# Two-byte halves of y made at the gating, with GpSimd subtracting and loading the first weights of the last projection

## The chip, the cores and the metric

The kernel runs on one core of a Trainium2 chip. The metric is device time in microseconds, the median of several executions.

## The reference

Two pre-norm residual layers over x (1024 tokens by 1024 features), then a last RMSNorm. Layer 0 is a gated linear recurrence, layer 1 an attention with a forget gate, 16 heads of 64. The change lies in layer 1:

```python
def fox_mixer(h, w_in, b_f, w_out):
    u = h @ w_in                       # q, k, v, gate (1024 each) and f_logit (16)
    cum = jnp.cumsum(jax.nn.log_sigmoid(f_logit), axis=1)
    ...
    logits = einsum(q, k) * scale + (cq - ck)      # causal
    p = jax.nn.softmax(logits, axis=-1)
    o = einsum(p, v)
    y = o * jax.nn.silu(gate)
    return y @ w_out                   # added to x, then rms_norm
```

## The kernel before

One function, `trunk`, writes the whole program; a scheduler with a timeline of its own then settles each engine's order. Features lie along the partitions (128 rows), tokens along the free dimension, in two halves of 512, called c = 0 and 1. Products of nearly four-byte accuracy are made by TensorE from pairs of narrower numbers: each operand is a high part (the number rounded) and a low part (what the rounding lost), and a product is three matmuls, high by high, low by high, high by low. In layer 1 the parts are two-byte (FP16) with scales worked out ahead.

Layer 0 takes the first 470 us or so and isn't touched. Layer 1 goes head by head (`for hd in range(HEADS)`, the loop behind `drain(fill)`); two heads make a pair, since 2 x 64 rows fill the partitions. In a head:

- `maxima(hd, c)` makes the logits `S` for blocks of 128 queries; VectorE adds the mask and takes the extreme (line 1086), ScalarE does the exponential and the high part of the probabilities `pp`, VectorE the low part (1099), and SyncE's queue transposes `pp` to `pT` by DMA (1101).
- `weigh(hd, c)` multiplies `pT` by the values into `O`, and ScalarE and VectorE put the sum into `yo` (1134), four-byte, two buffers by turns.
- `gated(hd, c)`, after the second head of a pair, multiplies `yo` by the gate `sg` on VectorE (1145). For pairs 0 to 5 the product goes to `kept_y`, twelve four-byte tiles under the tag `hl` (16 places); pairs 6 and 7 keep it in `yo`.

Between these, strings such as `"1..1..1..1..0.0"` say at each step whether the next piece is one of the attention (`0`, `1`), of the values (`v`, `w`) or of `fill` (`.`), a stream of large projections: `play(units)` makes units of 24 matmuls for keys, queries and gates. Each unit fills one of the two PSUM banks under the tag `g` (tiles `gps`), which is scaled by VectorE (783) and used: a gate unit by a tanh on ScalarE and a multiply on VectorE (1055, tile `sg`), a key or query unit by a copy and a subtract (909, tile `qkl`). The bank is free again after that.

From head 12 on `fill` holds the last gate units (`last_g`) and then the last projection. `partial(todo)` makes, for each of 8 blocks db of 128 output features and each half c, a unit of 18 matmuls `ops` over pairs 0 to 5; pairs 6 and 7 are added at the end in `turned`. A unit needs:

- the two-byte halves of `y`. `split_loaded` makes them from `kept_y` during the last gate unit and the first units: `split_16`, one scaled cast on ScalarE and one VectorE operation (1175) for each of the twelve tiles, into new places under the tag `hh`, the places of the normed input;
- the block's weights: `split_out(db)` loads them (256 KB and 128 KB) through `load16`, which shares three places `wf` (and SyncE's queue, line 69) with all other weights, and casts them with `cast16` (ScalarE, then VectorE at 738) into `w`;
- the residual block, loaded from DRAM by GpSimd's queue (1236) into the place that `home(c, db)` gives: `xh`, under `hl`, for c = 0; `xp` or `xh` elsewhere for c = 1. VectorE adds the product to it (1239). A copy of one element by GpSimd (1234) holds the next load back until the block before last has been added, and three `xp` blocks are stored again (1241).

`late()` loads and casts the weights of pairs 6 and 7, `turned` transposes the sum, adds the last products and applies the final norm (line 1305, tile `res`).

Of the kernel before, what the change touches and what calls it, by code (L numbers as in the profile page):

```python
# [11 lines left out]
F32 = mybir.dt.float32  # L12
F32R = mybir.dt.float32r
BF16 = mybir.dt.bfloat16
FP16 = mybir.dt.float16
TOP = 32768.0
AF = mybir.ActivationFunctionType
ALU = mybir.AluOpType

P = 128  # L20
SEQ = 1024
HALF = 512
KT = 8
# [20 lines left out]
def trunk(ctx: ExitStack, tc: tile.TileContext, xt, w0, wg, wo0, pc, gn, gf, w1, wv, wf, bf, wo1, out):  # L44
    nc = tc.nc
# [6 lines left out]
    hpool = ctx.enter_context(pool("hT", 16))  # L52
# [155 lines left out]
    with nullcontext(ExitStack()) as l0:  # L208
# [43 lines left out]
        first = ([], [])  # L252
        early = [weights(w0[0], lo_eng=nc.vector), weights(w0[NB], lo_eng=nc.gpsimd)]
        k = 0
# [315 lines left out]
        total_o, unit_o, scale_o, scale_y, inv_o, eps_o, most, gain = (outs[:, i : i + 1] for i in range(8))  # L570
# [100 lines left out]
        for h, cs in enumerate(halves):  # L671
            y = [tuple(z[:, cs] for z in p) for p in ys[-2:]]
# [3 lines left out]
            for d0 in range(0, KT, 4):  # L676
# [6 lines left out]
                for db, o in enumerate(pts, d0):  # L683
                    mm3(o, wl[db][1], y[1], False, True)
                    x = xs[h][db]
# [28 lines left out]
    with ExitStack() as l1:  # L714
# [7 lines left out]
        seen = [None]  # L722

        def load16(src, shape, b):

            wt = loaded(shape)
            for part, sl in src:
                fetch(wt[:, :, sl], part)
            return wt, b

        def cast16(wt, b, scale=None):

            scale = scales[:, b : b + 1] if scale is None else scale
            n = wt.shape[1]
            both = wpool.tile([P, 2, *wt.shape[1:]], FP16, tag=next(slots), name="w16")
            hi, lo = both[:, 0], both[:, 1]
            cast_last[0] = nc.scalar.activation(hi, wt, AF.Copy, scale=scale)
            nc.vector.scalar_tensor_tensor(lo, wt, scale, hi, ALU.mult, ALU.subtract)
            return [(hi[:, k], lo[:, k]) for k in range(n)]
# [144 lines left out]
        sgs = {}  # L884
        yos = {}
        y1 = [{}, {}]
        kept_y = [[hpool.tile([P, HALF], F32, tag="hl", name="y") for pair in range(6)] for c in range(2)]
        wo = {}

        kqw = {}  # L890
# [246 lines left out]
        def gated(hd, c, sub=slice(0, HALF)):  # L1137

            if hd % 2 == 0:
                return  # L1140
            pair = hd // 2
            yo = to = yos[pair, c][:, sub]
            if pair < 6:
                to = kept_y[c][pair][:, sub]
            nc.vector.tensor_tensor(
                to, yo, sgs[pair][:, c * HALF + sub.start : c * HALF + sub.stop], ALU.mult
            )
            if hd == 15:
                split_y(c, pair, yo, sub)

# [17 lines left out]
        def pair_of_y(c, pair):  # L1168
            both = hpool.tile([P, 2, HALF], FP16, tag="hh", name="y16")
            y1[c][pair] = both[:, 0], both[:, 1]  # L1170
            return y1[c][pair]

        def split_16(y, yh, yl):
            to_hi(yh, y, nc.scalar, scale=scale_y)
            nc.vector.scalar_tensor_tensor(yl, y, scale_y, yh, ALU.mult, ALU.subtract)
# [2 lines left out]
            yh, yl = (z[:, sub] for z in (pair_of_y(c, pair) if sub.start == 0 else y1[c][pair]))  # L1178
            split_16(y, yh, yl)

        def high_y(c):
            for pair in range(6):
                pair_of_y(c, pair)
            yield from ()

        def split_loaded(c):
            for pair in range(6):
                y = kept_y[c][pair]
                split_16(y, *y1[c][pair])
                if pair % 2:  # L1190
                    yield

        def beside(steps, first, more):

            for i, _ in enumerate(steps):
                if i >= first:
                    next(more, None)
                yield

        def split_out(db):  # L1200
            if db < KT and db not in wo:
                wo[db] = []
                for k, n in ((0, 4), (4, 2)):
                    wo[db] += cast16(*load16([(wo1[db, :, k : k + n], slice(0, P))], (n, P), None), scale_o)

        def first_out():
            split_out(0)
# [3 lines left out]

        def home(c, db):
            if c == 0:
                x = hpool.tile([P, HALF], F32, tag="hl", name="xh")
            elif db < 3:
                return rpool.tile([P, HALF], F32, tag="R", name="xp")
            elif db < 7:
                x = at.tile([P, HALF], F32, tag="wv", name="xh", bufs=4)
            else:
                x = at.tile([P, HALF], F32, tag="wvf", name="xh", bufs=1)  # L1220
            homes[c, db] = x
            return x
# [153 lines left out]
        for hd in range(HEADS):  # L1376
            pair = hd // 2
            if hd % 2 == 0:
                if hd < 12:
                    fill = play(next(fills))  # L1380
                elif hd == 12:
                    todo = [(db, c) for c in range(2) for db in range(2)]
                    todo += [(db, c) for db in range(2, KT) for c in range(2)]
                    splits = [split_loaded(c) for c in range(2)]
                    fill = chain(
                        play(next(fills)),
                        play(last_g[0]),
                        high_y(0),
                        first_out(),
                        beside(play(last_g[1]), 1, splits[0]),  # L1390
                        high_y(1),
                        beside(partial(todo), 3, splits[1]),
                        last_gains(),
                        turned(0, 0),
                        turned(0, 1),
                    )
            elif pair < 6:
                fill = play(next(fills))
            first, second = LAST if hd > 11 else START if hd == 0 else ORDER
            if hd in (4, 8):  # L1400
                first, second = OPEN
            if hd == HEADS - 1:
                first = "1..1.0.1.0.1..."
            side = chain(pieces(hd + 1, 0, 0), pieces(hd + 1, 0, 1)) if hd else iter(())
            run(first, weigh(hd, 0), maxima(hd, 1), fill=fill, side=side, vals=vals, wvals=wvals)
            drain(side)
            if hd == HEADS - 1:
                break
            if hd == 14:
                with tc.issue_after(seen[0].ins):  # L1410
                    split_y(1, 6, yos[6, 1])
            gated(hd, 0)
            side = chain(pieces(hd + 2, 1, 0), pieces(hd + 2, 1, 1))
            if hd == 14:
                side = chain(side, late())
            if hd % 4 == 3 and hd < 11:
                wvals, second = value_weights(hd // 4 + 2), TURN
            run(second, weigh(hd, 1), maxima(hd + 1, 0), fill=fill, side=side, vals=vals, wvals=wvals)
            if hd % 4 == 3 and hd < 11:
                drain(vals)  # L1420
                vals = values_beside(hd // 4 + 2)
            drain(side)
            gated(hd, 1)
            if hd == 13:
                with tc.issue_after(seen[0].ins):
                    split_y(0, 6, yos[6, 0])
            if hd < 12:
                drain(fill)
# [81 lines left out]
```

## Time and profile before

| | |
|---|---|
| median of 3 runs | 1020.6 us (1019.57 to 1020.7) |
| the profiled execution's own time | 1016.93 us |
| its span, first to last instruction | 1015.2 us |
| mean granted clock of TensorE | 0.999 |
| PE / DVE / ACT / POOL busy | 995.4 / 788.4 / 669.1 / 110.4 us |

PE is TensorE's matmuls, PEld its weight loads, DVE is VectorE, ACT ScalarE, POOL GpSimd, SP SyncE; a q behind the name is that engine's queue. An arrow to the left in a row reads "waits for" where two engines are named, and "made from" where two tiles are. L with a number is a line of the kernel; matmuls, ScalarE's operations and SyncE's loads are issued by helpers and carry the helper's line (72, 60, 69), so they are told apart by their tiles.

### The profile page before, as it was taken

The page shows a single profiled execution, that of the slowest core. Times are in us where ns is not written, and L with a number is a line of the kernel's source. Part 1 is how long each engine was busy: PE and PEld are TensorE (multiplying, and loading weights), DVE is VectorE, ACT ScalarE, POOL GpSimd, SP SyncE. Part 2 cuts the span into 40 slices and gives each one's busy share as a digit, 9 for nine tenths or more (in the row PEclk, how much of TensorE's full clock was granted, in tenths as well). Part 3 has the DMA queues.
Part 4 walks back from the last instruction along what each step waited for, and adds up shares of the span by engine and source line. Part 5 has one row for each costly group of instructions (what it writes and reads, how often), then busy time and mean ns, then how long its engine had stood idle before and what let it go on. Part 6 is the DMA issues. An engine that isn't in the chain of part 4 may idle for free. (4 is left out here: it accounts for less than half of the span.)

```text
span 1015.2 us, 15117 instructions
## 1 busy us (share of the span) xinstructions
PE 995.4 (98%) x5100; PEld 655.3 (65%) x5100; DVE 788.4 (78%) x1500; ACT 669.1 (66%) x1219; POOL 110.4 (11%) x104
## 2 busy tenths in 40 slices
PE   9999999999999999999999999999999999999997
PEld 6787778888888888776545555555555555444454
DVE  7689585586567557898687988988898878995875
ACT  8469855657657567576684667776667666873655
POOL 1310221222122122000200000000010000001200
PEclk9999999999999999999999999999999999999999
DMA  7211443243334333244366687977688677777954
GB/s 256 62 51 48 126 140 97 91 133 103 124 106 131 96 107 113 70 148 137 85 157 124 122 151 147 193 152 150 130 202 136 138 160 150 154 180 185 231 101 167
DMA packets 219629, 135.88 MB, mean 134 GB/s; under 512 B 162080, under 2 KB 186464, under 8 KB 219552
## 3 DMA queue, kind: packets, MB, share of 16 engines
q1 hardware_dynamic: 216912, 126.27, 51.5%
q0 software_dynamic: 2640, 8.65, 3.1%
q8 instruction: 40, 0.66, 0.3%
q14 instruction: 37, 0.30, 0.1%
HBM read 75.16 MB, written 9.37 MB: 83 GB/s over the span
## 5 line engine op out<-in xcount | busy, mean ns | idle before, releaser
L72 PE MATMUL gps<-h,w 128*128 128x512 f16 x1152 | 268.0, 379 | 0.0
L72 PEld LDWEIGHTS <-w 128*128 128x128 f16 x1440 | 139.9, 98 | 156.3 <-issue 6.8
L60 ACT ACTIVATE p<-p,m 128x128 f32<-128x128 f32 (+7 forms) x128 | 98.9, 772 | 84.1 <-DVE m L1086 75.4
L114 POOL TENSOR_TENSOR wl<-wf,wh 128x512 fp32r<-128x512 f32 x46 | 82.0, 1791 | 315.9 <-ACT wh L60 258.5
L1086 DVE CUSTOM_DVE_ANT_0 p<-S,mask,vsq 128x128 f32<-128x128 f32 (+7 forms) x128 | 103.6, 810 | 14.6 <-PE S L72 14.2
L1099 DVE SCALAR_TENSOR_TENSOR pp<-p,sums,pp 128x128 f16<-128x128 f32 (+7 forms) x128 | 103.4, 812 | 12.2 <-ACT pp L60 11.7
L60 ACT ACTIVATE pp<-p,sums 128x128 f16<-128x128 f32 (+7 forms) x128 | 97.9, 768 | 20.1 <-ACT p L60 14.4
L60 ACT ACTIVATE wsf<-wsf 128x512 f32<-128x512 f32 (+1 forms) x81 | 50.5, 625 | 60.5 <-DMA wsf<-in_w 33.0
L72 PEld LDWEIGHTS <-h 128*128 128x128 f16 x768 | 74.8, 98 | 21.0 <-ACT h L60 1.3
L72 PE MATMUL S<-T,U 128*128 128x512 f16 (+4 forms) x384 | 83.4, 327 | 0.1
L72 PE MATMUL ops<-yh,wh 128*128 128x512 f32 x192 | 77.2, 402 | 1.6 <-ACT yh L60 0.9
L72 PE MATMUL ups<-hh,wh 128*128 128x512 f32 x192 | 76.3, 398 | 1.0 <-ACT hh L60 0.8
L72 PE MATMUL ups<-hl,wh 128*128 128x512 f32 x192 | 76.2, 397 | 0.2 <-DVE hl L275 0.2
L72 PE MATMUL ops<-yh,wl 128*128 128x512 f32 x192 | 75.7, 394 | 0.8 <-DVE wl L114 0.8
L72 PE MATMUL ups<-hh,wl 128*128 128x512 f32 x192 | 75.6, 394 | 0.8 <-POOL wl L114 0.8
L72 PE MATMUL gps<-hh,wh 128*128 128x512 f32 x192 | 75.8, 395 | 0.0
L72 PE MATMUL gps<-hh,wl 128*128 128x512 f32 x192 | 75.5, 393 | 0.1
L72 PE MATMUL gps<-hl,wh 128*128 128x512 f32 x192 | 75.4, 393 | 0.0
L72 PE MATMUL ops<-yl,wh 128*128 128x512 f32 x192 | 74.5, 394 | 0.0
L413 DVE TENSOR_TENSOR x<-x,ops 128x512 f32<-128x512 f32 x80 | 53.7, 679 | 24.8 <-PE ops L72 24.4
L72 PE MATMUL ops<-y,w 128*128 128x512 f16 x288 | 67.5, 379 | 3.5 <-DVE sg L1055 2.2
L72 PE MATMUL vps<-wv,h 128*128 128x256 f16 x576 | 70.4, 273 | 0.0
(253 smaller groups left out, 1764.8 us busy)
## 6 DMA issues: line engine op xcount, KB each, us to landing
wf<-in_w SPq DMA_DIRECT2D x106, 256.0 KB
wsf<-in_w SPq DMA_DIRECT2D x48, 256.0 KB
wf<-in_wo SPq DMA_DIRECT2D x64, 128.0 KB
x<-in_xt SPq DMA_DIRECT2D x16, 256.0 KB
wsf<-in_wv SPq DMA_DIRECT2D x16, 256.0 KB
wsf<-in_wo SPq DMA_DIRECT2D x16, 256.0 KB
x1d<-x SPq DMA_DIRECT2D x16, 256.0 KB
T<-qkh SPq DMA_DIRECT2D x64, 64.0 KB
```

Source lines behind the costliest of these rows:

```text
L60: act[0] = op(*args, **kw)
L72: pe[0] = nc.tensor.matmul(*args, **kw)
L114: return eng.tensor_tensor(lo, src, f32(hi), ALU.subtract)
L413: nc.vector.tensor_tensor(x, x, pt, ALU.add)
L1086: nc.vector.tensor_tensor_reduce(p, S[:, :n], mask[:, SEQ - n :], unit_s[:, pair : pair + 1], -NEG, ALU.add, ALU.min, accum_out=m)
L1099: nc.vector.scalar_tensor_tensor(both[:, :, 1], p, r, both[:, :, 0], ALU.mult, ALU.subtract)
```

## The change

For pairs 0 to 5 the two-byte halves of `y` are made at once where the pair is gated. VectorE multiplies `yo` by the scale and the gate in place, ScalarE copies the result to the high half, and GpSimd subtracts to get the low half. `kept_y` is gone: the halves, together as large as one four-byte tile, lie in its places under `hl`. `high_y`, `split_loaded` and `beside` are gone.

The weights of the last projection for pairs 0 to 5 are loaded by GpSimd's queue into the four places under `hl` that are left (`load_out`): blocks 0 and 1 before head 12's pieces, block db + 2 when block db is cast. The residual blocks of c = 0 go under `hh`, the places of the normed input.

```diff
-        kept_y = [[hpool.tile([P, HALF], F32, tag="hl", name="y") for pair in range(6)] for c in range(2)]
+        for c, pair in itertools.product(range(2), range(6)):
+            y = hpool.tile([P, 2, HALF], FP16, tag="hl", name="y16")
+            y1[c][pair] = y[:, 0], y[:, 1]
...
-            yo = to = yos[pair, c][:, sub]
+            yo = yos[pair, c][:, sub]
+            g_ = sgs[pair][:, c * HALF + sub.start : c * HALF + sub.stop]
             if pair < 6:
-                to = kept_y[c][pair][:, sub]
-            nc.vector.tensor_tensor(
-                to, yo, sgs[pair][:, c * HALF + sub.start : c * HALF + sub.stop], ALU.mult
-            )
+                yh, yl = y1[c][pair]
+                nc.vector.scalar_tensor_tensor(yo, yo, scale_y, g_, ALU.mult, ALU.mult)
+                with tc.issue_after(seen[0].ins):
+                    to_hi(yh, yo, nc.scalar)
+                nc.gpsimd.tensor_tensor(yl, yo, yh, ALU.subtract)
+            else:
+                nc.vector.tensor_tensor(yo, yo, g_, ALU.mult)
...
+        raw_o = {}
+
+        def load_out(db):
+            if db < KT:
+                raw_o[db] = []
+                for k, n in ((0, 4), (4, 2)):
+                    wt = hpool.tile([P, n, P], F32, tag="hl", name="wof")
+                    nc.gpsimd.dma_start(wt, wo1[db, :, k : k + n])
+                    raw_o[db].append(wt)

         def split_out(db):
             if db < KT and db not in wo:
                 wo[db] = []
-                for k, n in ((0, 4), (4, 2)):
-                    wo[db] += cast16(*load16([(wo1[db, :, k : k + n], slice(0, P))], (n, P), None), scale_o)
+                for wt in raw_o.pop(db):
+                    wo[db] += cast16(wt, None, scale_o)
+                load_out(db + 2)
...
-                x = hpool.tile([P, HALF], F32, tag="hl", name="xh")
+                x = hpool.tile([P, HALF], F32, tag="hh", name="xh")
...
-                    splits = [split_loaded(c) for c in range(2)]
+                    for db in range(2):
+                        load_out(db)
                     fill = chain(
                         play(next(fills)),
                         play(last_g[0]),
-                        high_y(0),
                         first_out(),
-                        beside(play(last_g[1]), 1, splits[0]),
-                        high_y(1),
-                        beside(partial(todo), 3, splits[1]),
+                        play(last_g[1]),
+                        partial(todo),
```

TensorE's matmuls stand in the same order in both kernels. On VectorE, in head 12, from behind the scaling of the last gate unit but one to that unit's `sg`, there stood before (`y` with a number is a half being split, `w<-wf` a cast of weights):

```order
L1097 RECIPROCAL sums<-sums 128x1
L1175 SCALAR_TENSOR_TENSOR y_8857<-y,outs,y_8857 128x512
L1096 TENSOR_SCALAR sums<-sums 128x1
L1175 SCALAR_TENSOR_TENSOR y_8940<-y,outs,y_8940 128x512
L1175 SCALAR_TENSOR_TENSOR y_8941<-y,outs,y_8941 128x512
L1175 SCALAR_TENSOR_TENSOR y_8942<-y,outs,y_8942 128x512
L1097 RECIPROCAL sums<-sums 128x1
L738 SCALAR_TENSOR_TENSOR w_8865<-wf,outs,w_8865 128x256
L1175 SCALAR_TENSOR_TENSOR y_8943<-y,outs,y_8943 128x512
L738 SCALAR_TENSOR_TENSOR w_8993<-wf,outs,w_8993 128x512
L1175 SCALAR_TENSOR_TENSOR y_8944<-y,outs,y_8944 128x512
L1055 SCALAR_TENSOR_TENSOR sg_8804<-sg_8804,gps_8805 128x512
```

And now, from the scaling of that unit (`gps_8837`) to the `sg` of the last one; `w_9111` and `w_9114` are block 2's weights, `w_9176` and `w_9179` block 3's:

```order
L783 SCALAR_TENSOR_TENSOR gps_8837<-gps_8837,wsq,rs_3505 128x512
L1098 TENSOR_SCALAR sums<-sums 128x1
L1101 SCALAR_TENSOR_TENSOR pp<-p,sums,pp 128x2x128
L1099 RECIPROCAL sums<-sums 128x1
L1101 SCALAR_TENSOR_TENSOR pp<-p,sums,pp 128x3x128
L738 SCALAR_TENSOR_TENSOR w_9114<-wof,outs,w_9114 128x256
L1057 SCALAR_TENSOR_TENSOR sg_8836<-sg_8836,gps_8837 128x512
L1101 SCALAR_TENSOR_TENSOR pp<-p,sums,pp 128x4x128
L738 SCALAR_TENSOR_TENSOR w_9176<-wof,outs,w_9176 128x512
L783 SCALAR_TENSOR_TENSOR gps_8894<-gps_8894,wsq,rs_3506 128x512
L738 SCALAR_TENSOR_TENSOR w_9179<-wof,outs,w_9179 128x256
L1057 SCALAR_TENSOR_TENSOR sg_8836<-sg_8836,gps_8894 128x512
```

No `y` split is left there; weight casts of later blocks have moved up between the gate's steps. On GpSimd, from the end of layer 1's preparations to the first store of a residual block, there stood before:

```order
L1031 AFFINE_SELECT mask<-mask 128x1024
L813 DMA wvf<-in_wv 128x512 x11
L1236 DMA xh<-x1d 128x512 x2
L1236 DMA xp<-x1d 128x512 x2
L1241 DMA x1d<-xp 128x512
```

And now, from the low half of pair 5 in c = 0 (`y_3864`) on; `y_3870` is that of c = 1, `wof` the weights:

```order
L1151 TENSOR_TENSOR y_3864<-yo,y_3864 128x512
L1194 DMA wof<-in_wo 128x512
L1194 DMA wof<-in_wo 128x256
L1194 DMA wof<-in_wo 128x512
L1194 DMA wof<-in_wo 128x256
L1151 TENSOR_TENSOR y_3870<-yo,y_3870 128x512
L1234 DMA xh<-x1d 128x512
L1194 DMA wof<-in_wo 128x512
L1194 DMA wof<-in_wo 128x256
L1234 DMA xh<-x1d 128x512
L1194 DMA wof<-in_wo 128x512
L1194 DMA wof<-in_wo 128x256
```

The subtracts, the weight loads and the residual loads share one queue in this order, and each waits for its own place or input with the others behind it.

15 lines of the change are left out of this document (removed).

## The prediction

> **What bounds the kernel now.** I read the page first: its span and its line of busy times.
>
> ```profile
> span 1015.2 us, 15117 instructions
> PE 995.4 (98%) x5100; PEld 655.3 (65%) x5100; DVE 788.4 (78%) x1500; ACT 669.1 (66%) x1219; POOL 110.4 (11%) x104
> ```
>
> TensorE (PE) is busy for 98% of the span, so a change that leaves its instructions alone, as this one does, can give back at most the 20 us in which it stood still. The table by stretches says where those lie (length, then busy time and count of PE, weight load, VectorE, ScalarE, GpSimd; then clock, DMA share, GB/s).
>
> ```profile
> 530.00:880.00 350.00, 350.00 (x2075) 191.90 (x2074) 295.31 (x702) 236.65 (x460) 4.81 (x9) 1.00 0.75 151
> 880.00:905.00 25.00, 22.82 (x114) 10.47 (x113) 24.61 (x54) 19.96 (x38) 1.07 (x2) 1.00 0.63 143
> 905.00:935.00 30.00, 30.00 (x155) 14.09 (x154) 20.95 (x50) 14.03 (x27) 5.91 (x12) 1.00 0.93 215
> 935.00:962.00 27.00, 25.59 (x125) 11.33 (x124) 21.28 (x50) 17.81 (x32) 5.38 (x12) 1.00 0.91 208
> 980.00:1016.00 36.00, 28.02 (x177) 16.84 (x174) 20.39 (x47) 18.11 (x49) 0.00 (x0) 0.96 0.42 137
> ```
>
> From 530 to 880, heads 1 to 11 nearly all, PE never stops. Then 2.2 us are missing in 880 to 905, where VectorE (DVE) is full (24.61 of 25), and 1.4 us in 935 to 962. The waits of PE from 880 on name them (total, times, longest):
>
> ```profile
> PE ops L72 <- DVE sg L1055: 2.2, 2, 1.3
> PE turn L72 <- DVE res L1305: 1.2, 1, 1.2
> PE ops L72 <- DVE xh L1239: 0.8, 2, 0.7
> PE ops L72 <- DVE sums L1096: 0.5, 1, 0.5
> ```
>
> The first place, in order of time, with DVE's and PE's rows of the timeline:
>
> ```profile
> 881.61 1.39 DVE L1175 SCALAR_TENSOR_TENSOR y<-y,outs,y 128x512 f16<-128x512 f32 x2
> 886.70 0.74 DVE L783 SCALAR_TENSOR_TENSOR gps<-gps,wsq,rs 128x512 f32<-128x512 f32 x1
> 888.15 2.06 DVE L1175 SCALAR_TENSOR_TENSOR y<-y,outs,y 128x512 f16<-128x512 f32 x3
> 892.58 0.67 DVE L1055 SCALAR_TENSOR_TENSOR sg<-sg,gps 128x512 f32<-128x512 f32 x1
> 893.30 2.75 PE L72 MATMUL ops<-y,w 128*128 128x512 f16 x12 [0.85 <-DVE sg L1055]
> 898.61 0.67 DVE L1055 SCALAR_TENSOR_TENSOR sg<-sg,gps 128x512 f32<-128x512 f32 x1
> 899.33 1.46 PE L72 MATMUL ops<-y,w 128*128 128x512 f16 x6 [1.33 <-DVE sg L1055]
> ```
>
> The first two units of the last projection (`ops`) want the two PSUM banks of the last two gate units; those come free when DVE has made `sg`, and DVE makes `sg` late because the `y` splits of line 1175 stand in front. The second place:
>
> ```profile
> 931.06 7.71 SPq L69 DMA_DIRECT2D wf<-in_wo  x6
> 936.43 0.72 ACT L60 ACTIVATE w<-wf,outs 128x512 f16<-128x512 f32 x1 [6.41 <-DMA wf<-in_wo]
> 937.18 0.75 DVE L738 SCALAR_TENSOR_TENSOR w<-wf,outs,w 128x512 f16<-128x512 f32 x1 [4.75 <-ACT w L60]
> 939.33 0.75 DVE L1239 SCALAR_TENSOR_TENSOR xh<-xh,outs,ops 128x512 f32<-128x512 f32 x1
> 940.12 1.46 PE L72 MATMUL ops<-y,w 128*128 128x512 f16 x6 [0.66 <-DVE xh L1239]
> ```
>
> ScalarE (ACT) stood 6.4 us for a weight load out of SyncE's queue, DVE behind it 4.75 us, and what DVE then did late (`xh`, the reciprocal's scale) kept PE waiting 0.7 and soon after 0.5 us; a last 0.1 us on `xh` follows near 960, also behind a late load.
>
> **The change, part by part.** PE's own order is the same in both kernels; only its waits can change. The rows for what is removed and added:
>
> ```profile
> L1175 DVE SCALAR_TENSOR_TENSOR y<-y,outs,y x12: 721/733/734, 881.6 to 894.8; 128x512 f16<-128x512 f32 x12
> L1145 DVE TENSOR_TENSOR y<-yo,sg x12: 681/684/693, 567.5 to 861.4; 128x512 f32<-128x512 f32 x12
> L60 ACT ACTIVATE y<-y,outs x12: 707/711/723, 880.0 to 891.9; 128x512 f16<-128x512 f32 x12
> L114 POOL TENSOR_TENSOR wl<-wf,wh x46: 1284/1298/3311, 8.9 to 395.9; 128x512 fp32r<-128x512 f32 x46
> ```
>
> **DVE's splits.** Twelve times 0.733, 8.8 us, go from 881.6 to 895.5, where DVE is the late engine. Into the space come casts of weights that stood later: the two parts of blocks 2 and 3 are now ahead of the second `sg`, part of block 3's formerly behind it. Even at 0.75 each (the 937.18 row), four are 3.0 us, and the two of block 2 stood there before. DVE wins 5.8 us or more on a stretch whose waits are 0.85 and 1.33 us. Both waits go: 2.2 us.
>
> **The gating.** The multiply of line 1145 becomes a scaled one: between 0.684 (its own row) and 0.75 (the two-operand casts); I take 0.733, so 12 x 0.05 = 0.6 us of DVE in 530 to 880, where it idles 54.7 us (350 - 295.3) and PE waits for nothing. ACT's twelve copies (0.711 each, 8.5 us) are moved, not added; ACT idles 113 us there. Queued behind such a copy, which waits for DVE's product, are the next exponential and softmax cast; DVE and then PE would feel that only after the softmax lead, which no row shows used up. Nothing is charged.
>
> **GpSimd's subtracts.** Twelve of 1.3 us (at most 3.3, the longest row), 16 to 40 us, on an engine with 4.81 us of work in these 350. Queued behind them are the loads of `wvf`; the subtract starts right after ACT's copy, while the next such load must first wait for DVE's cast, so 0 to 1 us each is lost, on a load for which ACT waits rather than PE. What they might do to DVE is seen in the first layer, where GpSimd runs the same operation:
>
> ```profile
> L379 DVE TENSOR_TENSOR ti<-ti,m x13: 681/1217/2186, 73.0 to 413.0; 128x1024 f32<-128x1024 f32 x11, 128x512 f32<-128x512 f32 x2
> ```
>
> One DVE multiply with both inputs in SBUF lasted 0.97 us longer than the median, and GpSimd's subtract up to 2.0 longer (3311 - 1298). So the price to DVE is 0 to 0.97 us each, 0 to 11.6 us in all, against 54.7 us of idle time; to PE I charge 0. [...]
>
> **Weights by GpSimd.** Sixteen loads leave SyncE's queue; ACT's 6.4 us wait was for one of them. Blocks 0 and 1 are now asked for before head 12, into free places, and block n+2 when block n is cast. What such a load costs stands in the rows of GpSimd's own loads (issue min/median/max; KB and median landing):
>
> ```profile
> L813 POOL DMA_DIRECT2D wvf<-in_wv x12: 536/536/683, 489.6 to 751.8; - x12
> xh<-x1d POOLq DMA_DIRECT2D x13, 256.0 KB, 4.4
> 879.42 0.73 DVE L738 SCALAR_TENSOR_TENSOR w<-wf,outs,w 128x512 f16<-128x512 f32 x1
> ```
>
> Issuing adds 16 x 0.54 = 8.6 us to a queue that is busy 12.4 us in 880 to 962. The tightest is block 2: block 0's place is free at 880.15, the load lands 4.4 later at 884.6. Then ACT casts it, does an exponential, two softmax casts, block 2's second part and the gate's tanh, at 0.71 each as an estimate 4.3 us: 888.9; DVE's `sg` makes 889.6, where PE wants the bank at 892.45. Cover 2.9 us. Later blocks are asked for two units and more ahead, so the waits of 0.7, 0.5 and 0.1 us go: 1.3 us.
>
> [...]
>
> **Places.** The residual blocks `xh` of the first half now wait for the normed input instead of sitting loaded early:
>
> ```profile
> 752.28 1.06 POOL L1236 DMA_DIRECT2D xh<-x1d  x2
> 878.61 2.75 PE L72 MATMUL gps<-h,w 128*128 128x512 f16 x12
> 884.65 2.75 PE L72 MATMUL gps<-h,w 128*128 128x512 f16 x12
> 883.00 0.66 DVE L909 TENSOR_TENSOR qkl<-gps,qkh 128x512 f16<-128x512 f32 x1
> ```
>
> The last reader of the first place is the unit at 878.6, so the load can land by about 884, for use at 899. A near one is the bank that the unit at 884.65 takes: DVE's `qkl` frees it at 883.66. Ahead of it two splits (1.39) go and three casts come (1.4 by the short form's size, 2.2 at 0.73 each): 0 to 0.8 us later, cover 1.0. Charged 0, bound 0.3.
>
> **Sum.** 2.2 + 1.3 = 3.5 us. The 1.2 us on `res` behind 980 belongs to the last stage, which stays. The profiled execution took 1016.93 us (span 1015.2 and 1.7 around it); 1016.93 - 3.5 = 1013.4. The three runs have a median of 1020.6, 3.7 above that; PE's work is the same, so I carry the difference over: 1020.6 - 3.5 = 1017.1.
>
> **The rivals.** Half the relief: The 2.2 us go, but around 935 another step is late (GpSimd serves its loads, stores and one-element copies in one order, and each copy waits for DVE), or `qkl` costs its 0.3: gain 1.1 to 2.2, 1018.4 to 1019.5. For it: DMA engines are 0.91 to 0.93 busy there; against it: DVE idles 9 of 30 us in 905 to 935.
>
> **The port.** If a third of the 0.97 us comes through to PE at each subtract, 12 x 0.32 = 3.9 us eat the gain: 1021.0, within 0.2%. Against it: PE shows no wait in 350 us with DVE at 84%.
>
> **No net change.** DVE's queue fills with casts that wait, and `sg` is as late as before: 1020.6.
>
> **Loads too late: slower.** If GpSimd's loads land later than ACT reaches them, each of blocks 2 to 7 repeats what one load did at 936: 0.7 + 0.5 = 1.2 us of PE. Six make 7.2, less 3.5: 1024.3. It decides from a landing of over 7.3 us (4.4 + 2.9); the rows say 4.4, though among DMA engines that are less crowded than the 0.91 to 0.93 here. [...]
>
> **More.** If the order around 980 also loses its 1.2 us on `res`: 1015.9.
>
> **How the numbers follow.** About 0.2%, 2.0 us, is what a measurement of this kernel can tell from no change. Forecast 0.58; more 0.07; half the relief 0.16, counted as within, since most of it lies under 2.0; port 0.06; no net change 0.05; loads too late 0.08. Faster 0.65, same 0.27, slower 0.08. The range holds the forecast, more and half the relief (0.81), from 1015.9 to 1019.5, and 0.5 us more at each end, half of the 1.1 us over which the three runs spread: 1015.4 to 1020.0.
>
> **What would show it.** Right: PE has no wait on `sg` and at most 0.3 us on `xh` and `sums` after 880; line 1175 keeps only its five `yo` splits; ACT waits for no `wof` over 2 us; PE still never stops from 530 to 880. Wrong: a wait of PE on softmax steps before 880 (the port); ACT waits of several us on `wof` with PE waits behind them (loads); PE waits of the same size on other DVE results (no net change).

## The result and the profile after

| kernel | median (range), runs | ratio to before, 95% interval |
|---|---|---|
| before, beside it | 1019.45 us (1018.58 to 1020.7), 6 | |
| after | 1015.34 us (1014.44 to 1016.53), 6 | 0.9958 [0.9945, 0.9971] |
| after, a second time | 1017.28 us (1014.41 to 1020.51), 11 | 0.9983 [0.9972, 0.9994] |
| after, a third time | 1017.21 us (1012.76 to 1018.35), 12 | 0.9985 [0.997, 0.9999] |

The change is faster in all three comparisons, by 0.42%, 0.17% and 0.15% (4.3, 1.7 and 1.5 us); these are small differences, but each interval ends under 1. In the third the medians lie only 0.4 us apart (1017.64 and 1017.21), the means 1.5. A fourth measurement stands under "The queue, the subtracts and the lead". One execution of before in the third comparison took 2620.76 us and is left out of its ratio. The first median lies 0.06 us below the predicted range. The profiled execution of after took 1014.72 us, 2.2 us less than that of before. Its page begins:

```profile
span 1013.0 us, 15148 instructions
PE 994.3 (98%) x5100; PEld 654.2 (65%) x5100; DVE 782.4 (77%) x1488; ACT 668.1 (66%) x1219; POOL 133.3 (13%) x132
```

Its table by stretches (the columns are those of the prediction's table):

```profile
530.00:880.00 350.00, 349.45 (x2070) 191.15 (x2069) 294.88 (x697) 242.07 (x471) 19.82 (x23) 1.00 0.75 151
880.00:905.00 25.00, 25.00 (x126) 11.64 (x125) 21.28 (x52) 15.28 (x30) 6.43 (x12) 1.00 1.05 230
905.00:935.00 30.00, 28.48 (x147) 13.29 (x146) 21.63 (x51) 16.46 (x32) 7.84 (x17) 1.00 0.89 184
935.00:962.00 27.00, 27.00 (x139) 12.48 (x137) 19.45 (x45) 14.13 (x27) 6.55 (x14) 1.00 0.84 187
```

TensorE has no gap any more in 880 to 905 and in 935 to 962, where 2.2 and 1.4 us were missing. VectorE has 3.7 us of slack in the first of these. But 1.5 us are missing in 905 to 935, where before had none. The waits of TensorE behind 880 are now two:

```profile
PE O L72 <- issue: 1.5, 1, 1.5
PE turn L72 <- DVE res L1303: 1.2, 1, 1.2
```

The waits on `sg`, `xh` and `sums` are gone, that on `res` is as it was, and a wait on the attention product `O` is new. Three rows of the timeline, of SyncE's queue, of TensorE and of ScalarE, say what it is:

```profile
910.31 3.84 SPq L1103 DMA_TRANSPOSE pT<-pp  x1
920.02 0.59 PE L72 MATMUL O<-pT,v 128*128 128x512 f16 x2 [1.52 <-issue]
920.03 0.72 ACT L60 ACTIVATE pp<-p,sums 128x512 f16<-128x512 f32 x1 [1.61 <-DMA pT<-pp]
```

The first product of head 13's second half needs the four transposes of that half. The last of them was started at 910.31; ScalarE, which waits for the same transfer to give back its `pp` buffer, is released at 920.03, within 0.01 us of TensorE. So the wait that the page can only call "issue" ends when that transpose lands, 9.7 us after its start. In before the same transpose landed in at most 6.5 us, since TensorE took up the product without a wait:

```profile
913.43 3.43 SPq L1101 DMA_TRANSPOSE pT<-pp  x1
919.91 0.59 PE L72 MATMUL O<-pT,v 128*128 128x512 f16 x2
```

### The profile page after: what moved, and what is told of

It reads as the page before. It is cut to its first block, busy times and chain, and to the rows that moved or that the text cites. A ratio compares the mean times of both kernels' runs of the same rounds, so it can differ in the third digit from the quotient of the medians.

```text
span 1013.0 us, 15148 instructions
## 1 busy us (share of the span) xinstructions
PE 994.3 (98%) x5100; PEld 654.2 (65%) x5100; DVE 782.4 (77%) x1488; ACT 668.1 (66%) x1219; POOL 133.3 (13%) x132
## 4 chain that ended last, share of the span: by engine, by line
PE 73%; issue 8%; DVE 7%; DMA 6%; ACT 3%; POOL 1%; SPq 0%; ACTq 0%; DVEq 0%; POOLq 0%
PE gps L72 28%; PE ops L72 16%; PE ups L72 9%; PE vps L72 6%; PE S L72 6%; PE O L72 5%; DMA wf<-in_w 2%; PE gate L72 2%; DMA wvf<-in_wv 1%; POOL wl L114 1%; PE turn L72 1%; DMA wsf<-in_wo 1%; DVE h L665 1%; DVE w L738 1%; ACT L60 1%
```

## The experiments

Each group of up to four ran on one chip, beside the kernel before on that chip: 1019.47 us in the first group (27 runs), 1018.37 in the second (35), 1018.11 in the third (14), 1017.64 in the fourth (33).

### Before and after again

The files are unchanged.

> The kernel before, once more, for its profile. If the profiled execution of before stands for the others, TensorE's waits behind 880 us add up to 4.6 to 5 us as there (2.2 on sg, 1.3 on xh and sums, 1.2 on res) and the time is near 1017. If that execution was a lucky one, the waits are 1 to 4 us longer, the time is 1018.5 to 1020.7 as in the timed runs, and the profile shows which wait is longer. Against itself the ratio should be 1 within 0.0015.

> The changed kernel once more. Its six times fall in two groups, 1014.4 to 1014.7 and 1016.0 to 1016.5. If the new wait of 1.5 us on a transposed block (O, near 920) is what differs, a profile without it has a span 1.5 us shorter than 1013.0, and one of the slower group shows it twice or longer. If it is always there, the two groups have another cause. Ratio to the kernel before 0.9945 to 0.997.

Before: 1019.09 us, ratio 0.9998 [0.9986, 1.0011]; after: 0.9983, as in the table. The executions of before spread from 1015.78 to 1021.07 us, those of after from 1014.41 to 1020.51. So three runs within 1.1 us, as there were ahead of the prediction, say little on the spread. In this profile of before (own time 1015.78) the waits on `sg` and `xh` are 1.8 and 1.4 us; in this one of after (1014.41) TensorE waits 1.4 us on `O` and 0.7 on `xh`. Both are the shortest executions of their kernel in this group. So the first doesn't say which wait is longer in the others, and the wait on `O`, which is there even in a short execution, doesn't tell the two groups of after's first six times apart.

### Each part alone

The halves at the gating, with the weights loaded by SyncE as in before:

```
-                for wt in raw_o.pop(db):
-                    wo[db] += cast16(wt, None, scale_o)
-                load_out(db + 2)
+                for k, n in ((0, 4), (4, 2)):
+                    wo[db] += cast16(*load16([(wo1[db, :, k : k + n], slice(0, P))], (n, P), None), scale_o)
...
-                    for db in range(2):
-                        load_out(db)
```

> The halves are made at the gating, by ScalarE and GpSimd, but the weights are loaded by SyncE through the three shared places as before. If the two parts of the change pay each for its own wait: the 2.2 us on sg go, the long ScalarE wait for wf (6 us near 930) and the waits behind it stay: 2.2 us faster, ratio 0.9978. If everything comes from the halves: the whole 4.1 us, ratio 0.996. If the loads are what counts: ratio above 0.999.

The weights by GpSimd, with `y` kept whole and split in head 12 and the residual blocks of c = 0 under `hl`, both as in before (against the changed kernel, the main lines):

```
-        for c, pair in itertools.product(range(2), range(6)):
-            y = hpool.tile([P, 2, HALF], FP16, tag="hl", name="y16")
-            y1[c][pair] = y[:, 0], y[:, 1]
+        kept_y = [[hpool.tile([P, HALF], F32, tag="hl", name="y") for pair in range(6)] for c in range(2)]
...
-                        play(last_g[1]),
-                        partial(todo),
+                        beside(play(last_g[1]), 1, splits[0]),
+                        high_y(1),
+                        beside(partial(todo), 3, splits[1]),
```

> The halves are split in head 12 as before, the weights come by GpSimd into the spare places. If the two parts pay each for its own wait: the 2.2 us on sg stay, 1.3 us behind 935 go, ratio 0.9987. If everything comes from the loads: ratio 0.996. If the residual blocks, which now share the places of the kept y with the loads, come late, a new wait of TensorE on xh appears and the ratio is above 1.

Measured: the halves alone 1021.96 us, ratio 1.0027 [1.0015, 1.004]; the loads alone 1024.58 us, ratio 1.005 [1.0034, 1.0067]. Each part alone is slower than before, and both together are faster: they don't pay for two separate waits. First the halves alone, by the timeline of SyncE's queue, ScalarE, VectorE and TensorE:

```profile
891.54 0.57 SPq L69 DMA_DIRECT2D wf<-in_wo  x1
894.04 0.51 ACT L60 ACTIVATE w<-wf,outs 128x256 f16<-128x256 f32 x1 [5.82 <-DMA wf<-in_wo]
894.59 0.48 DVE L738 SCALAR_TENSOR_TENSOR w<-wf,outs,w 128x256 f16<-128x256 f32 x1 [5.64 <-ACT w L60]
897.00 5.34 SPq L69 DMA_DIRECT2D wf<-in_wo  x4
900.48 0.72 ACT L60 ACTIVATE w<-wf,outs 128x512 f16<-128x512 f32 x1 [1.63 <-DMA wf<-in_wo]
901.26 0.39 PE L72 MATMUL ops<-y,w 128*128 128x512 f16 x1 [2.51 <-ACT w L60]
```

VectorE is free of the splits, and what it wins it spends on waiting: the weights come from SyncE's queue behind transposes and head loads. ScalarE stands 5.82 us for the first piece and VectorE 5.64 behind it; ScalarE stands 1.63 us more for the next one, and TensorE 2.51 behind that. But the splits are not the only difference to before, where SyncE's queue has these loads earlier:

```profile
885.63 1.55 SPq L69 DMA_DIRECT2D wf<-in_wo  x3
```

The scheduler settled that queue's order anew. This run doesn't tell apart what the missing splits cost and what the later loads.

With the loads alone it is the other way round (VectorE, then TensorE):

```profile
894.17 2.07 DVE L1175 SCALAR_TENSOR_TENSOR y<-y,outs,y 128x512 f16<-128x512 f32 x3
897.48 0.68 DVE L1055 SCALAR_TENSOR_TENSOR sg<-sg,gps 128x512 f32<-128x512 f32 x1
898.21 5.28 PE L72 MATMUL ops<-y,w 128*128 128x512 f16 x12 [3.78 <-DVE sg L1055]
929.06 0.59 PE L72 MATMUL O<-pT,v 128*128 128x512 f16 x2 [2.76 <-DMA pT<-pp]
```

The casts of weights are ready early and stand in VectorE's order ahead of `sg`, together with the splits; VectorE has no idle time from 880 to 900, and `sg` is made at 897.48, where TensorE has waited 3.78 us. The third row shows more: twelve matmuls took 5.28 us, not the 2.75 of the row at 893.30 in before. TensorE ran at about half its pace there (the mean granted clock of this execution is 0.995, that of before's 0.999; see the hardware below), and on these twelve alone that costs 2.5 us on top of the wait. The fourth row is the wait on `O` again, here put down to the transpose by the profile itself: the early loads alone bring it. A wait of 1.5 us on `xh` is there too (at 969.06), but not, as was expected, because a residual block is late: VectorE stands 6.20 us ahead of it, behind ScalarE's wait of 6.29 us for a weight load of pairs 6 and 7.

### The queue, the subtracts and the lead

Three kernels of this group change one line each of the changed kernel, and the fourth two:

```
spare_by_sync     -  nc.gpsimd.dma_start(wt, wo1[db, :, k : k + n])
                  +  nc.sync.dma_start(wt, wo1[db, :, k : k + n])
vector_subtract   -  nc.gpsimd.tensor_tensor(yl, yo, yh, ALU.subtract)
                  +  nc.vector.tensor_tensor(yl, yo, yh, ALU.subtract)
subtract_twice    -  nc.gpsimd.tensor_tensor(yl, yo, yh, ALU.subtract)
                  +  for _ in range(2):
                  +      nc.gpsimd.tensor_tensor(yl, yo, yh, ALU.subtract)
one_ahead         -  load_out(db + 2)
                  +  load_out(db + 1)
                  -  for db in range(2):
                  +  for db in range(1):
```

> The whole change, but the sixteen loads of the last projection's first weights are issued by SyncE, at the same places of the program and into the same spare places. Theory (what matters is that a load is issued two blocks ahead of its use, into a place that is free): about as the change measured so far, ratio to before 0.996 to 0.999, no wait of ScalarE on these weights over 3 us and no wait of TensorE behind one. Rival (what matters is the queue: on SyncE's queue the loads stand behind transposes that wait for VectorE): the wait of the run with the halves alone comes back, ScalarE waiting 4 us or more for a piece, TensorE 2 us or more behind it, ratio 1.001 or more.

Measured: 1021.02 us, ratio 1.0014 [0.9994, 1.0035]. In the profile (an execution of 1018.13 us) ScalarE waits for `wof` four times, 9.1 us in all, against once and 2.5 us in after. TensorE does not wait behind these: its longest wait is again on `O`, and longer.

```profile
ACT w L60 <- DMA wof<-in_wo: 9.1, 4, 4.4
PE O L72 <- issue: 3.7, 1, 3.7
```

So the early place alone does not do it; the queue matters too. By which way the twelve executions, half of them over 1020.9 us, are longer is shown only for this one: the 3.7 us at `O` and the half clock behind them (0.50 from 923 to 926 us).

> The whole change, but the low halves of y are subtracted by VectorE, not by GpSimd. Theory (between 565 and 865 us VectorE has the room): twelve subtractions of about 0.7 us each add some 8.2 us to VectorE's 295 of 350 us there, VectorE then busy 303, nothing of it on TensorE: as the change within 1 us, TensorE's waits before 880 within 0.5 us of the change's. Rival (GpSimd's part is what frees VectorE at the gatings): a wait of TensorE of over 0.5 us behind a gating, and 1 to 3 us longer than the change.

Measured: 1017.56 us, ratio 0.9981 [0.9967, 0.9996], as the change in its second and third measurement. The twelve subtracts last 0.683 us each on VectorE, and TensorE waits for none of them. The profiled execution took 1022.3 us, and ScalarE's and TensorE's timeline shows one way to such a time:

```profile
756.60 0.72 ACT L60 ACTIVATE wv<-wvf,wsq 128x512 f16<-128x512 f32 x1 [5.68 <-DMA wvf<-in_wv]
758.80 0.52 PE L72 MATMUL gps<-h,w 128*128 128x512 f16 x1 [3.88 <-ACT w L60]
759.59 3.89 PE L72 MATMUL gps<-h,w 128*128 128x512 f16 x11 [0.27 <-DVE w L738]
```

One value-weight load (line 813, in both kernels) took 8.1 us to land, where the median of the three in that stretch is 4.4; ScalarE, then TensorE stood for it, and the clock fell (0.50 from 759 to 762 us). So the time bears out the theory and this profile doesn't: TensorE waits 5.8 us from 520 to 880 for weights, against 0.4 in the changed kernel. Whether the subtracts on VectorE have a part in the late load is open.

> The whole change with each of GpSimd's twelve subtractions issued twice (the second writes the same numbers again). Theory (GpSimd's work costs VectorE nothing here): GpSimd 14 us busier, every subtraction still 1.15 to 1.21 us, VectorE's steps beside them as long as before, the time as the change within 1 us. Rival (GpSimd and VectorE hold each other up at memory): VectorE's steps beside the subtractions up to 1.2 us longer, twelve of them, of which some reaches TensorE: 2 us or more over the change.

Measured: 1018.3 us, ratio 0.9992 [0.9979, 1.0006]: by the ratios 0.7 to 0.9 us over the change's second and third measurement, which the intervals do not tell apart. GpSimd is 15.0 us busier (148.3), VectorE 1.3 (783.7), and its gating products beside the subtracts last 743 to 751 ns. Nothing of it reaches TensorE, which is busy 349.64 of the 350 us from 530 to 880. The wait on `O` is 3.1 us in this execution. Yet the two engines do hold each other up, if by little. The subtracts' row, and two of VectorE's line 1101 on 640 columns, beside a subtract in the changed kernel (after):

```profile
L1152 POOL TENSOR_TENSOR y<-yo,y x24: 1147/1159/1777, 568.3 to 865.4; 128x512 f16<-128x512 f32 x24
582.75 0.88 DVE L1101 SCALAR_TENSOR_TENSOR pp<-p,sums,pp 128x640 f16<-128x640 f32 x1
696.00 1.15 DVE L1101 SCALAR_TENSOR_TENSOR pp<-p,sums,pp 128x640 f16<-128x640 f32 x1
```

Four of the second subtracts last 1.62 to 1.78 us, against the row's median of 1.16, each begun while VectorE ran line 1101. In after one step of line 1101 began 0.5 us before a subtract ended and lasted 1.15 us in place of 0.88, and one more, begun 0.3 us before an end, 1.02. So the lengthening that the rival named is there; that memory is where the two engines meet was not shown, and its price, 2 us or more, is not there.

> The whole change, but a block's weights are loaded one block ahead of their use, not two, so that one block's loads, not two, are under way ahead of the first projection block and the DMA engines are less crowded from 880 to 905 us. Theory (the lead is what pays, and the crowd costs little): a load lands in about 5.6 us and a block is used every 5 to 6 us, so ScalarE waits for the weights again, TensorE behind it by 1 to 4 us in all, ratio to before 0.999 to 1.004. Rival (the crowd is what holds the transposes up): the wait of 1.5 us on the attention product at about 920 us goes, no new one comes, and the time is 1 to 2 us under the change's.

Measured: 1017.07 us, ratio 0.998 [0.9966, 0.9993]. But this edit changes nothing that runs. As built, every engine has the changed kernel's instructions, in the same order and at the same addresses; only the tiles' numbers differ. So the loads of two blocks still go out together, in after and here:

```profile
851.54 2.14 POOL L1194 DMA_DIRECT2D wof<-in_wo  x4
854.60 2.14 POOL L1194 DMA_DIRECT2D wof<-in_wo  x4
```

This is a fourth measurement of the changed kernel, and neither theory on the lead was tested. Its profile has 1.3 us on `O` and 0.6 on `xh`; ScalarE waits 2.8 us for `wof`, and a load lands in 5.4 us.

### What the new wait is

```
quiet_loads       +  kept_o = []
                  ...
                  -  if db < KT:
                  +  if 5 < db < KT:
                  +      raw_o[db] = list(kept_o)
                  +  elif db < KT:
                  ...
                  +      kept_o[:] = raw_o[db]
later_product,    -  LAST = "1..1..1..1..0.0", "1..1.1..1..0..0.0.0"
later_again       +  LAST = "1..1..1..1..0.0", "1..1.1..1...0.0.0.0"
later_by_two      +  LAST = "1..1..1..1..0.0", "1..1.1..1....0.0.00"
before_later         later_product's LAST in the kernel before
```

In `LAST` a 0 is a step of the attention product, a 1 a row block of scores, and a dot six matmuls of the projection. The kernel quiet_loads leaves out the weights of blocks 6 and 7 and takes block 5's again; all its other instructions stand in the changed kernel's order on every engine. In later_product and later_again only TensorE's order differs.

> The whole change, but the weights of the last projection's last two blocks of this stage (blocks 6 and 7) aren't loaded: their products use block 5's weights again, so that four loads, 768 KB in all, which the change issues from 907 to 916 us, are left out. Theory (the transfers of that stretch hold up the transposes for head 13's attention product): the transpose that the changed kernel's product waits for to 920 us lands 2 us or more sooner, that wait of 1.5 us (3.1 and 3.7 us in two other runs) is under 0.5 us, and the time is 1 to 3 us under the change's. Rival (the transposes are late by VectorE and by their own queue, whatever else is moved): the wait stays over 1 us and the time as the change within 1 us.

Measured: 1013.52 us (1013.15 to 1014.55), ratio 0.9952 [0.9933, 0.997]. TensorE's waits from 880 to 1016:

```profile
PE turn L72 <- DVE res L1307: 1.2, 1, 1.2
PE ops L72 <- DVE xh L1241: 0.6, 1, 0.6
```

The last transpose of head 13 in SyncE's queue, and the product in TensorE's timeline:

```profile
909.83 3.07 SPq L1103 DMA_TRANSPOSE pT<-pp  x1
917.88 0.59 PE L72 MATMUL O<-pT,v 128*128 128x512 f16 x2
```

The wait on `O` is gone, and TensorE takes up the product 8.05 us after the transpose's start, not 9.5 us or more as in the changed kernel's four profiles. All six executions lie within 1.4 us. Without these four loads the transposes are in time: the transfers that the change moved to GpSimd's queue hold up the ones on SyncE's.

> The whole change, and of heads 12 to 14 the first step of the second half's attention product stands one step of six matmuls (1.3 us) later in TensorE's order, with the work beside it brought forward by as much. Theory (TensorE comes to head 13's product before its transposed weights have landed, and now and then this costs 3 us and then half the clock): the wait at about 920 us shrinks by 1.3 us, to nothing in a profile like the change's, long waits become rarer, and the median is 1 to 2.5 us under the change's. Rival (the wait only moves to what is brought forward: weights or sums that aren't there yet): a new wait of 1 us or more on the projection's weights, time as the change within 1 us or longer.

> The kernel with head 13's attention product one step of six matmuls later, once more and beside the changed kernel itself. Theory (the later product hides 1.3 us of a wait of 1.5 to 3.7 us, and so keeps it under the length at which the clock falls): ratio to before 0.994 to 0.997, 1 to 2.5 us under the changed kernel on the same chip. Rival (its first measurement was luck): within 0.7 us of the changed kernel.

Measured: 1014.99 us, ratio 0.9955 [0.9937, 0.9973], and again 1015.2 us, ratio 0.9974 [0.9964, 0.9984], 2.0 us by the medians and 1.1 by the means under the changed kernel on the same chip in the same group (1017.21). The waits on `O` are 0.8 and 1.1 us in the two profiles. The gain over before holds in both; that over the changed kernel is likely but not settled, since the two intervals against before overlap.

> The whole change, and of heads 12 to 14 the first step of the second half's attention product two steps (2.6 us) later, with none left between its last two steps. Theory (the wait has 0.8 us left with one step): no wait at that product in a profile, and the median 0 to 1 us under the kernel with one step. Rival (the step that is brought forward is missed elsewhere: the attention steps that end the head now come without work between them): a wait of 1 us or more at the end of the product or at the next head's first step, time 0.5 us or more over the kernel with one step.

Measured: 1014.34 us (1011.23 to 1016.47), ratio 0.9965 [0.9951, 0.9979], as the kernel with one step within the intervals. The `O` wait is gone, and 1.5 us on `xh` have come in its place, in 935 to 962:

```profile
PE ops L72 <- DVE xh L1237: 1.5, 1, 1.5
PE turn L72 <- DVE res L1303: 1.2, 1, 1.2
```

Its median is 2.9 us under that of the changed kernel in the same group.

> The changed kernel once more, beside the kernel with the product one step later. Theory (its executions are of two kinds: the wait on head 13's attention product is 1.5 us and no more, or it is 3 us or more, and TensorE then runs at half its clock for some 3 us): executions between 1014 and 1020 us, the median 1 us or more above that of the kernel with the later product. Rival (the two measurements so far, 0.9958 and 0.9983, differ by chip and chance alone): the same median as the kernel with the later product within 0.7 us.

Measured: 1017.21 us, ratio 0.9985 [0.997, 0.9999]: 2.0 us over the median of the kernel with the later product beside it. The profiled execution waits 2.4 us on `O`. Of the 2.2 us by which it is longer than after's first (1016.96 against 1014.72) these are 0.9; 1.25 were lost before TensorE's first scores of layer 1 (at 510.02 us, in the other at 508.77). Of its executions five took 1012.76 to 1015.82 us and seven 1016.96 to 1018.35. That the longer ones wait over 3 us on `O` and then run at half the clock was seen in two neighbours (spare_by_sync, subtract_twice), not in this kernel itself.

> The kernel before with the same order as the kernel with the later product (one step of six matmuls moved ahead of the second half's attention product in heads 12 to 14), and nothing of the change. Theory (the wait on the product at 920 us is made by the change, which brings TensorE there earlier and fills the DMA engines; before has no such wait): no gain, the median within 1 us of before, TensorE's waits on the second halves' factors and on the partial sums as in before, 3 to 5 us together. Rival (the later product is a gain by itself, the change apart): 2 us or more under before.

Measured: 1018.37 us, ratio 1.0 [0.9983, 1.0017]. The later product gives nothing without the change, and the waits are those of before: `sg` 2.0, `xh` 1.6, none at the product. The new wait is the change's own.

### Two more executions of before

> The kernel before, for one more profiled execution. Theory (executions differ because now and then TensorE stands for 2.4 us or more at one wait, and then runs at half its clock for some 3 to 6 us): if its own time is 1018.5 us or more, one wait from 880 us on is 2.4 us or longer and the clock is under 0.95 in the stretch behind it; if it is under 1017 us, no wait is. Rival (the difference is spread over the span): a long execution shows the waits of the short ones, under 2 us each, and longer busy times in all stages.

> The kernel before, for one more profiled execution, with the same expectations as of the look ahead of it: own time 1018.5 us or more with a wait of 2.4 us or longer and a lower clock behind it, or under 1017 us without one; by the rival, a long execution without such a wait.

The two took 1019.14 and 1020.42 us, and the theory falls: no wait from 880 on is 2.4 us or longer. (These 2.4 us are the author's estimate; what followed waits of 2.36 to 3.88 us stands under the hardware below.) The first one's waits of TensorE and ScalarE's wait behind which they stand:

```profile
PE ops L72 <- DVE xh L1239: 3.1, 2, 2.0
PE ops L72 <- DVE sg L1055: 1.8, 2, 1.3
PE ops L72 <- DVE sums L1096: 0.5, 1, 0.5
```

```profile
937.87 0.72 ACT L60 ACTIVATE w<-wf,outs 128x512 f16<-128x512 f32 x1 [7.80 <-DMA wf<-in_wo]
```

The second has `xh` 2.3, `sg` 2.0 and `sums` 0.5. So the late loads out of SyncE's queue cost TensorE 3.6 and 2.8 us in these, 1.3 in the execution that the prediction read. The 2.3 us between are about what the first one is longer (1019.14 - 1016.93 = 2.2). Of the second one's 3.5 us they are 1.5, and 1.3 were lost before the first scores (at 510.28 us, in the other at 508.97). What made up the 1.3 us was not shown. The rival, a difference that is spread out, is nearer to the second, the theory to neither.

## Why the prediction was wrong, point by point

**The mechanism was right in the main.** The waits on `sg` and `sums` are gone, line 1175's twelve splits too, TensorE waits its 1.2 us on `res` as said, and from 530 to 880 it stands still for little (0.55 us, in before for none). Two of the signs failed: `xh` keeps 0.7 and 0.6 us in two of four profiles, over the 0.3 allowed, and ScalarE waits 2.5 to 3.0 us for one `wof` load in each, over the 2 allowed; TensorE doesn't feel that.

**The step that failed** is the one that starts from "1020.6 us" and reads "PE's work is the same, so I carry the difference over: 1020.6 - 3.5 = 1017.1", with a low end "0.5 us more at each end, half of the 1.1 us over which the three runs spread". The miss of 1017.1 - 1015.34 = 1.76 us has two parts. The median of three runs was high: six runs gave 1019.45, 1.15 us less, and the later groups 1017.64 to 1019.47. And the gain in that comparison was 4.11 us by the medians, 0.61 more than the sum. The difference between a profiled execution and the median isn't a constant that both kernels share, since part of it is made of the very waits that the change removes: `sg`, `xh` and `sums` come to 3.5 us in the execution that was read, and 3.2, 5.4 and 4.8 in the three others, a mean of 4.2. The first scores, too, begin anywhere from 507.45 to 510.60 us in the eighteen profiles, so that part of the difference is settled before the change begins.

**The term that the sum lacked** is the wait on `O`: 1.5, 1.4, 2.4 and 1.3 us in four profiles of the changed kernel, and in two of them 0.7 and 0.6 on `xh` besides, a mean of 2.0. The prediction looked for what would be late next on VectorE and on the weights, and not on SyncE's transposes, although it had the row of DMA engines 0.91 to 0.93 busy. 4.2 - 2.0 = 2.2 us is near the mean of the four measured gains, 2.4 (4.3, 1.7, 1.5, 2.0). So the forecast of 3.5 stands between the first measurement and the later ones; a sum with both terms right would have given less, and a range with the executions' own spread would have held all four medians. That the later three, 1017.28, 1017.21 and 1017.07, lie within 0.2 us of 1017.1 is luck: the starting value was 1.1 to 3.0 us above before's medians beside them, and the gain too large by about as much.

**The two waits are not separate items.** The sum added 2.2 for the splits and 1.3 for the loads. Alone the parts lose 2.8 and 5.1 us. With the splits gone and the weights still from SyncE, VectorE has 5.64 us to spare and stands, and the weights are late; with the weights early and the splits still there it has no idle time, and `sg` is late. That removing one exposes the other is how the two traces read; it isn't shown apart from the queue's new order in the first, and from the wait on `O` in the second.

**Gating and subtracts, right in size.** After's rows of line 1148, of the high half and of GpSimd's subtracts (count, ns min/median/max, from and to):

```profile
L1148 DVE SCALAR_TENSOR_TENSOR yo<-yo,outs,sg x12: 744/747/752, 567.4 to 862.2; 128x512 f32<-128x512 f32 x12
L60 ACT CAST y<-yo x12: 602/618/619, 568.1 to 864.2; 128x512 f16<-128x512 f32 x12
L1151 POOL TENSOR_TENSOR y<-yo,y x12: 1148/1157/1210, 568.8 to 864.9; 128x512 f16<-128x512 f32 x12
```

The product costs 0.063 us more, not 0.05; the subtract 1.16, not 1.3, with 0.06 us between the median and the longest. Where the two engines met, steps of both were longer: in after two of VectorE's last 0.27 and 0.14 us longer beside a subtract, and with the subtracts issued twice four of these last 0.46 to 0.62 us longer.

**The loads, off in size, hidden all the same.** They land in 5.6 us (3.8 to 8.0), not 4.4, as the rows of DMA issues (KB, median landing) and of line 1194 show:

```profile
wof<-in_wo POOLq DMA_DIRECT2D x8, 256.0 KB, 5.7
wof<-in_wo POOLq DMA_DIRECT2D x8, 128.0 KB, 5.6
L1194 POOL DMA_DIRECT2D wof<-in_wo x16: 536/536/553, 851.5 to 915.4; - x16
```

1.2 to 1.3 us more than the prediction took, within its cover of 2.9, though one took 8.0, over the 7.3 from which it counted loads as too late; ScalarE waits 2.5 us for one, TensorE not at all. The issues of 536 to 553 ns are no longer than those of before. Why the loads land later isn't shown; the DMA engines are busier from 880 to 905 than in before (a share of 1.05 against 0.63).

**The rivals.** "Half the relief" came nearest to the later two measurements, by another way than it named: a new wait of 1.3 to 2.4 us, at the transposes. Its point about DMA engines that are busy there was the right one. "Loads too late" is what happens to the halves alone, from SyncE's queue. "The port", the rival by which a third of what a subtract costs VectorE reaches TensorE: two steps of VectorE were longer, 0.4 us together, and nothing of it reached TensorE; that a port is what the two engines share was not shown.

## What to carry to other kernels

Where two stalls lie in one stretch, one engine's surplus work may be filling another's wait: price the parts together, and test each alone before calling one useless. When a change moves loads to a second queue to get them in early, look at what the first queue's transfers then lose (here the last transpose of head 13 took 9.7 us to its reader, and 8.05 at most with four of the loads left out), and give the consumer of those more work ahead of it; here one step of six matmuls brought forward took about half of that wait, and 1.1 to 2.0 us in the one comparison beside the change. Make sure that an edit changes the instructions that run before its time is read as an answer. Read a sum of sub-microsecond waits from several profiled executions, not from one, and take the range from the executions' spread.

## What the runs showed of the hardware

A standstill of TensorE cost a second time in five of these profiles. The stretches of the halves alone, of the third run of after, and of the loads alone (length, TensorE's busy time and count, clock, DMA share, GB/s):

```profile
901.00:902.00 1.00, 0.39 (x1) 0.80 0.17 64
902.00:903.00 1.00, 0.96 (x3) 0.50 0.02 3
903.00:904.00 1.00, 1.00 (x4) 0.50 0.39 128
904.00:905.00 1.00, 1.00 (x3) 0.50 0.92 178
905.00:906.00 1.00, 1.00 (x7) 0.99 1.12 189
```

```profile
922.00:923.00 1.00, 0.69 (x4) 1.00 1.41 335
923.00:924.00 1.00, 1.00 (x6) 1.00 0.84 81
```

```profile
928.00:929.00 1.00, 0.00 (x0) 1.00 1.75 335
929.00:930.00 1.00, 0.94 (x5) 1.00 0.53 98
```

After the wait of 2.51 us in the halves alone the clock is at half for 3.4 us (0.4 + 3.0 + 0.02), three or four matmuls per us instead of six, a loss of 1.7 us. After a wait of 2.36 us in the third run of after, and after one of 2.76 us in the loads alone, it stays at 1.00 in the rows above. The waits of 3.11 us (subtract_twice), 3.66 (spare_by_sync) and 3.88 (vector_subtract) were followed by 3.4 us at half, and behind that of 3.78 (loads_only) twelve matmuls took 5.28 us in place of 2.75. So 2.51 us were followed by the half clock and 2.76 us, as far as the rows reach, were not: the length of the wait alone does not sort these. What does was not shown.

Transfers of one queue held up those of another by 1.5 us and more: head 13's last transpose took 9.5 to 11.3 us from its start to where its reader went on with the early weight loads under way, and 8.05 at most with four of them left out.
